# Two weight chunks side by side: gate and up products in turn into two PSUM tiles

## The chip, the core and the metric

The kernel runs on one core of a Trainium2 chip, as one launch. The metric is the device time of an execution in microseconds (us). Five engines run their own instruction streams and wait for each other by semaphores: TensorE (PE in the profile; PEld is its loading of weights), VectorE (DVE), ScalarE (ACT), GpSimd (POOL) and SyncE (SP), which here issues the weight loads from HBM. Matrix products are summed in PSUM tiles, which ScalarE and VectorE read.

## The reference

One inference step of a two-layer backbone over 384 tokens (256 latent, 128 context) of width 1024. Each layer is a feed-forward, a mixing block (a gated MLP over chunks of tokens beside differential attention) and a second feed-forward; each of the three is modulated by scales, shifts and gates that come from a conditioning vector.

```python
def swiglu(h, w13, w2):
    gate, up = jnp.split(h @ w13, 2, axis=-1)
    return (jax.nn.silu(gate) * up) @ w2

mod = jax.nn.silu(cond) @ w_mod[l] + b_mod[l]
sh1, sc1, gt1, sh2, sc2, gt2, sh3, sc3, gt3 = jnp.split(mod, N_MOD, axis=-1)
h = rmsnorm(x, g_norm[l, 0]) * (1.0 + sc1) + sh1
x = x + 0.5 * gt1 * swiglu(h, ffn1_w13[l], ffn1_w2[l])
...
h = rmsnorm(x, g_norm[l, 2]) * (1.0 + sc3) + sh3
x = x + 0.5 * gt3 * swiglu(h, ffn2_w13[l], ffn2_w2[l])
```

D_FF is 2816, 22 columns of 128; a layer runs for the context under one conditioning vector and for the latents under another.

## The kernel before

Everything is kept transposed: 128 features on the partitions, 384 tokens along the free dimension, 8 such blocks for a width of 1024. All weights come in chunks of 128 x 1024 floats (512 KB), one DMA each (L149) into one of seven `raw` buffers. To keep precision in TensorE's fast float format, each operand is split in a high and a low half: for weights ScalarE writes the high half `whi` (L180) and VectorE the low half `wlo` (L183), four buffers of each; activations are held in the same way. A 128-deep step of a product is then three matmuls into the same PSUM tile (`mm3`, L232 to L234): high by high, low weight by high, high weight by low.

The program is a list of jobs. A job is a generator that yields after each such step; the driver `step` takes them one after another and after each yield runs what was deferred (`run_later`): the low half of a weight chunk four steps after its high half, the low half of an activation one step after. The order in which the jobs issue is the order of every engine's stream.

A feed-forward is such a list. First some leading columns, in groups that also prepare the normalised input (`start_group` in the very first, `lead` in the others), then for each of the other gate and up columns (chunks c = 4 to 43 in the first feed-forward, 8 to 43 in the others) one `col_job`: it fetches its chunk, asks for the split of the chunk three further on, runs 8 steps (24 matmuls of 384 columns) into one PSUM tile out of four (`ps_mm`), and evacuates it. The evacuation of a gate column is a Silu on ScalarE (L713) into `t`; that of an up column multiplies `t` by the PSUM tile on VectorE (L732) and splits the product (copy on ScalarE L408, low half on VectorE L411). Then 22 jobs of w2 chunks follow, which sum eight output columns over 22 steps each and update `x`.

Beside the matmuls the kernel computes the conditioning for later stages, on VectorE. A piece (`mod_piece`, one of the nine 1024-wide parts) takes ten jobs: 0 to 7 read one `raw` chunk each and add it to two accumulators (job 0: L437, the others L439, two instructions each), job 8 reduces both (L445, tile `red`), and job 9 begins with a small matmul on TensorE that reads `red` into the tile `ms` (L450) and then writes the result with VectorE (L454). These jobs are put between the column jobs by `mods.put`: in three of the four feed-forwards 26 of them are spread over the chunks c = 8 to 43 and 14 more follow in w2, one per job; in the last one 10 are spread. A `mods` job issues its instructions at once and yields nothing.

Of the kernel before, what the change touches and what calls it, by code (L numbers as in the profile page):

```python
# [15 lines left out]
P = 128  # L16
D = 1024
KD = 8
NT = 384
# [21 lines left out]
def hybrid_step(  # L41
# [5 lines left out]
    T, V, S, G = nc.tensor, nc.vector, nc.scalar, nc.gpsimd  # L47
# [5 lines left out]
    def ps_mm():  # L53
        return pp.tile([P, 512], F32, tag="mm", name="mm", bufs=4)

    def tmp(w=NT):
        return sp.tile([P, w], F32, tag="t", name="t", bufs=5)
# [28 lines left out]
    def duo(p):  # L86

        return tuple(slot(2 * p + n, [P, KD, NT], F32R) for n in range(2))
# [21 lines left out]
    split_of = {}  # L110
    st = {"loaded": 0, "done": 0, "split": 0, "job": 0, "cur": None}
# [41 lines left out]
    def raw_done(key):  # L153
        del raw_of[key]
        gone.add(key)
        while st["done"] < st["loaded"] and order[st["done"]] in gone:
            st["done"] += 1
        load_next()
# [3 lines left out]
    def defer(fn, n):  # L162
        later.append([n, fn])

    def run_later(n=1):

        for e in later:
            e[0] -= n
        while later and later[0][0] <= 0:
            later.pop(0)[1]()  # L170

    def split_upto(c):
        c = min(c, len(chunks) - 1)
        while st["split"] <= c:
            i = st["split"]
            key = chunks[i]
            raw = raw_of[key]
            hi = sp.tile([P, 1024], F32R, tag="whi", name="whi", bufs=W_BUFS)
            lo = sp.tile([P, 1024], F32R, tag="wlo", name="wlo", bufs=W_BUFS)
            S.activation(out=hi, in_=raw, func=AF.Copy)  # L180

            def low(hi=hi, lo=lo, raw=raw, key=key):
                V.tensor_tensor(out=lo, in0=raw, in1=hi.bitcast(F32), op=ALU.subtract)  # L183
                raw_done(key)
            defer(low, LO_LAG)
            split_of[i] = (hi, lo)
            st["split"] += 1

    def w_get(c):
        if c >= st["split"] - 1:  # L190
            split_upto(c)
            run_later(99)
        split_upto(c + W_BUFS - 1)
        return split_of.pop(c)
# [36 lines left out]
    def mm3(ps, w_hi, w_lo, r_hi, r_lo, first, last):  # L231
        T.matmul(ps, lhsT=w_hi, rhs=r_hi, start=first, stop=False)  # L232
        T.matmul(ps, lhsT=w_lo, rhs=r_hi, start=False, stop=False)  # L233
        T.matmul(ps, lhsT=w_hi, rhs=r_lo, start=False, stop=last)  # L234

    def col_job(key, rhs, evac, n=NT, beside=()):

        def gen(c):
            hi, lo = w_get(c)
            ps = ps_mm()  # L240
            r_hi, r_lo = rhs()
            for kt in range(KD):
                sl = slice(kt * P, (kt + 1) * P)
                mm3(ps[:, :n], hi[:, sl], lo[:, sl], r_hi[:, kt, :], r_lo[:, kt, :], kt == 0, kt == KD - 1)
                for at, f in beside:
                    if at == kt:
                        f()
                yield
            evac(ps[:, :n])
        Job([key], gen)  # L250

    def lead_group(keys, evacs, l, i):


        def gen(c):
            n = len(keys)
            split_upto(c + n)
            run_later(99)
            ws = [split_of.pop(c + e) for e in range(n)]
            pss = [ps_mm() for _ in range(n)]  # L260
            r_hi, r_lo = rhs_u()
            seq = [(e, kt) for kt in range(5) for e in range(n)]
            seq += [(e, kt) for e in range(n) for kt in range(5, KD)]
            for at, (e, kt) in enumerate(seq):
                if at == 6:
                    norm_stats()
                if at == 14:
                    norm_bcast()
                sl = slice(kt * P, (kt + 1) * P)
                hi, lo = ws[e]  # L270
                mm3(pss[e][:, :NU], hi[:, sl], lo[:, sl], r_hi[:, kt, :], r_lo[:, kt, :], kt == 0, kt == KD - 1)
                if kt == KD - 1:
                    evacs[e](pss[e][:, :NU])
                    split_upto(c + n + 1 + e)
                yield
        Job(keys, gen)
# [130 lines left out]
    def split_act(dst_hi, dst_lo, src, lag=1):  # L407
        S.activation(out=dst_hi, in_=src, func=AF.Copy)  # L408

        def low():  # L410
            V.tensor_tensor(out=dst_lo, in0=src, in1=dst_hi.bitcast(F32), op=ALU.subtract)  # L411
        if lag:
            defer(low, lag)
        else:
            low()
# [199 lines left out]
    def normed(ps, out):  # L615

        b = tiny(2, "yb")
        V.tensor_copy(out=b, in_=ps[:, NT:NU])
        V.tensor_tensor(out=out, in0=ps[:, 0:NT], in1=nst["rb"], op=ALU.mult)
        return b  # L620
# [75 lines left out]
    def ffn(l, i, w13, w2, mods, after, n13):  # L696
        g = {}
        pc_sh, pc_gt = 3 * i, 3 * i + 2
        first = (l, i) == (0, 0)

        def g_tile(f):
            b = f // 8
            if b not in g:
                g[b] = duo(role["ZXW"[b]])
            return g[b][0][:, f % 8, :], g[b][1][:, f % 8, :]

        s_of = {}

        def gate_evac(f, u):
            def e(ps):  # L710
                s = s_of[f] = tmp()
                if not u:
                    S.activation(out=s, in_=ps, func=AF.Silu)  # L713
                    return
                b = normed(ps, s)
                for n, s0, s1 in TOK:
                    S.activation(out=s[:, s0:s1], in_=s[:, s0:s1], func=AF.Silu, bias=b[:, n:n + 1])
            return e

        def up_evac(f, u):  # L720
            def e(ps):
                s = s_of.pop(f)
                hi, lo = g_tile(f)
                if u:
                    t = tmp()
                    b = normed(ps, t)
                    for n, s0, s1 in TOK:
                        V.scalar_tensor_tensor(
                            out=s[:, s0:s1], in0=t[:, s0:s1], scalar=b[:, n:n + 1], in1=s[:, s0:s1],
                            op0=ALU.add, op1=ALU.mult)  # L730
                else:
                    V.tensor_tensor(out=s, in0=s, in1=ps, op=ALU.mult)  # L732
                split_act(hi, lo, s)
            return e

        n_u = 0 if first else 8
        n_0 = 4 if first else n_u
        keys, evs = [], []
        for f in range(NFF):
            keys += [(w13, l, f, 0), (w13, l, f, 1)]  # L740
            evs += [gate_evac(f, 2 * f < n_u), up_evac(f, 2 * f < n_u)]
        if first:
            start_group(keys[:n_0], rhs_h, evs[:n_0], make_h0(l, i, pc_sh))
        else:
            Job([], lambda c: iter_once(turn))
            lead(keys[:n_0], evs[:n_0], l, i, pc_sh)
        spread = 2 * NFF - 8
        for c in range(n_0, 2 * NFF):
            col_job(keys[c], rhs_h, evs[c])
            if first and c in (n_0, n_0 + 4):  # L750
                Job([], lambda c, f=small_loads if c == n_0 else lambdas: iter_once(f))
            if c >= 8:
                e = c - 8
                mods.put((e + 1) * n13 // spread - e * n13 // spread)

        pst = {}

        def mk(ci):
            def gen(c):
                hi, lo = w_get(c)  # L760
                for t in range(8):
                    dt, kt = divmod(ci * 8 + t, NFF)
                    if kt == 0:
                        pst["ps"] = ps_mm()
                    ps = pst["ps"]
                    sl = slice(t * P, (t + 1) * P)
                    a_hi, a_lo = g_tile(kt)
                    mm3(ps[:, :NT], hi[:, sl], lo[:, sl], a_hi, a_lo, kt == 0, kt == NFF - 1)
                    if after is None and (dt, kt) == (KD - 1, 12):
                        final_sums(0)  # L770
                    yield
                    if kt == NFF - 1:
                        update_x(l, pc_gt, dt, ps[:, :NT], after)
            return gen
        for ci in range(NFF):
            Job([(w2, l, ci // 2, ci % 2)], mk(ci))
            if ci < 16:
                mods.put()
        assert not mods.todo
# [345 lines left out]
    def iter_once(f):  # L1125
        f()
        return iter(())
# [157 lines left out]
```

## Time and profile before

| | |
|---|---|
| time, median of 3 runs | 1919.38 us (1918.47 to 1919.88) |
| the profiled execution's own time | 1918.23 us |
| its span, first to last instruction | 1916.2 us |
| mean granted TensorE clock | 0.997 |
| TensorE busy | 1903.4 us, 99% of the span |
| VectorE busy | 1308.7 us, 68% |
| ScalarE busy | 789.7 us, 41% |
| GpSimd busy | 198.5 us, 10% |
| weight chunks split (whi, wlo) | 424 |
| three-fold steps (L232, L233, L234) | 3136 of each |

The share of busy time of TensorE is from overlapping matmul records, whose ends are modelled; what a matmul costs is therefore read from the distance between the starts of neighbours. In the rows of the timeline the first number is the start of an instruction in us from the start of the span, the second its duration; in brackets stands how long its engine was idle before it and what ended that. In the table by windows a row has, for each engine, busy time and the number of instructions, then the granted TensorE clock, the DMA engines' busy share and GB/s. In the list of waits a row has the total, how often, and the longest.

### The profile page before, as it was taken

How to read it: one execution, taken by the hardware profiler on the slowest of the kernel's cores; microseconds unless marked ns; L12 is line 12 of the kernel's file. 1: busy time of each engine (PE TensorE's matmuls, PEld its weight loads, DVE VectorE, ACT ScalarE, POOL GpSimd, SP SyncE). 2: the span in 40 equal slices, each digit the busy share in tenths (PEclk: the TensorE clock that was granted, in tenths of full speed). 3: DMA queues.
4: the chain of work that ended last, by engine and by line, in shares of the span. 5: the costliest groups of instructions: out<-in, count | busy, mean ns of one | idle time of the engine just before them, and what ended most of it. 6: DMA issues, size and time to landing. Idle time of an engine off the chain costs nothing.

```text
span 1916.2 us, 28408 instructions
## 1 busy us (share of the span) xinstructions
PE 1903.4 (99%) x11024; PEld 1849.4 (97%) x11024; DVE 1308.7 (68%) x1948; ACT 789.7 (41%) x1412; POOL 198.5 (10%) x399
## 2 busy tenths in 40 slices
PE   8999999999999999999999999999999999999998
PEld 7999999889999999999999999998899999999998
DVE  5677885777656768778768779668766546655543
ACT  4433334445553444333334333354555534433332
POOL 0000003101221031000040000050022200400000
PEclk9999999999999999999999999999999999999999
DMA  8666663643335536566536656546433333354430
GB/s 331 197 200 194 219 207 128 214 131 112 98 100 173 162 112 201 189 197 223 181 109 221 192 192 223 170 137 200 123 111 103 102 123 130 111 172 157 154 110 34
DMA packets 91719, 308.69 MB, mean 161 GB/s; under 512 B 10816, under 2 KB 17600, under 8 KB 90816
## 3 DMA queue, kind: packets, MB, share of 16 engines
q1 hardware_dynamic: 90864, 306.17, 49.0%
q8 instruction: 87, 1.43, 0.3%
q10 hardware_dynamic: 720, 0.70, 0.1%
q14 instruction: 48, 0.39, 0.1%
HBM read 303.16 MB, written 3.67 MB: 160 GB/s over the span
## 4 chain that ended last, share of the span: by engine, by line
PE 98%; DMA 1%; DVE 0%; ACT 0%; issue 0%; DVEq 0%; ACTq 0%
PE mm L232 29%; PE mm L233 28%; PE mm L234 28%; PE mm L388 2%; PE mm L390 2%; PE mm L389 2%; PE sc L1009 2%; PE mm L1067 1%; PE tp L1050 1%; DMA S<-in_w_mod 1%; PE tp L835 1%; DMA gnorm<-in_g_norm 0%; PE ms L1096 0%; PE sc L301 0%; PE tp L640 0%; DMA cond<-in_cond 0%
## 5 line engine op out<-in xcount | busy, mean ns | idle before, releaser
L232 PE MATMUL mm<-S,whi 128*128 128x384 f32 (+1 forms) x3136 | 1063.8, 339 | 1.2 <-ACT S L560 1.2
L233 PE MATMUL mm<-S,wlo 128*128 128x384 f32 (+1 forms) x3136 | 1054.2, 336 | 0.2 <-DVE wlo L183 0.2
L234 PE MATMUL mm<-S,whi 128*128 128x384 f32 (+1 forms) x3136 | 1048.7, 334 | 0.0
L183 DVE TENSOR_TENSOR wlo<-raw,whi 128x1024 fp32r<-128x1024 f32 x424 | 520.6, 1229 | 239.9 <-ACT whi L180 239.2
L232 PEld LDWEIGHTS mm<-S,whi 128*128 128x128 f32 x3136 | 589.5, 188 | 14.0 <-issue 10.0
L234 PEld LDWEIGHTS mm<-S,whi 128*128 128x128 f32 x3136 | 588.8, 188 | 0.4 <-DVE S L563 0.4
L233 PEld LDWEIGHTS mm<-S,wlo 128*128 128x128 f32 x3136 | 587.6, 187 | 0.8 <-DVE wlo L183 0.6
L180 ACT ACTIVATE whi<-raw 128x1024 fp32r<-128x1024 f32 x424 | 445.5, 1052 | 199.6 <-PE mm L234 116.5
L439 DVE SCALAR_TENSOR_TENSOR acc<-raw,scond,acc 128x1024 f32<-128x1024 f32 x224 | 277.3, 1280 | 0.0
L408 ACT ACTIVATE S<-t 128x384 fp32r<-128x384 f32 x144 | 74.1, 523 | 329.7 <-DVE t L732 241.3
L509 POOL TENSOR_TENSOR yr<-yv,nhalf 128x3 f32<-128x3 f32 x9 | 9.6, 1062 | 1344.0 <-DVE yv L529 1016.6
L411 DVE TENSOR_TENSOR S<-t,S 128x384 fp32r<-128x384 f32 x144 | 83.8, 590 | 34.6 <-ACT S L408 34.6
L732 DVE TENSOR_TENSOR t<-t,mm 128x384 f32<-128x384 f32 x76 | 42.1, 554 | 77.8 <-PE mm L234 77.8
L713 ACT ACTIVATE t<-mm 128x384 f32<-128x384 f32 x76 | 37.3, 491 | 137.5 <-PE mm L234 137.5
L388 PE MATMUL mm<-whi,S 128*128 128x512 f32 x192 | 77.3, 403 | 0.0
L390 PE MATMUL mm<-whi,S 128*128 128x512 f32 x192 | 75.2, 392 | 0.0
L389 PE MATMUL mm<-wlo,S 128*128 128x512 f32 x192 | 75.1, 391 | 0.0
L577 POOL TENSOR_SCALAR t<-t,amod,modT 128x256 f32<-128x256 f32 x80 | 67.3, 850 | 4.2
L502 ACT ACTIVATE t<-x 128x384 f32<-128x384 f32 x44 | 22.9, 526 | 98.3 <-DVE x L627 98.3
L1100 DVE SCALAR_TENSOR_TENSOR S<-ms,sublng,S 128x128 fp32r<-128x128 f32 (+1 forms) x32 | 13.4, 418 | 65.3 <-ACT S L1099 65.3
L1026 ACT ACTIVATE e<-sc,ym 128x384 f32<-128x384 f32 (+1 forms) x96 | 47.7, 508 | 20.0 <-DVE ym L1016 20.0
L627 DVE SCALAR_TENSOR_TENSOR x<-mm,modT,x 128x256 f32<-128x256 f32 x96 | 35.6, 413 | 28.3 <-PE mm L234 28.0
(150 smaller groups left out, 1144.0 us busy)
## 6 DMA issues: line engine op xcount, KB each, us to landing
raw<-in_ffn_w SPq DMA_DIRECT2D x264, 512.0 KB, 4.2
raw<-in_w_mod SPq DMA_DIRECT2D x132, 512.0 KB, 4.6
raw<-in_w_in SPq DMA_DIRECT2D x112, 512.0 KB, 3.8
raw<-in_w_branch_a SPq DMA_DIRECT2D x16, 512.0 KB, 3.7
raw<-in_w_branch_b SPq DMA_DIRECT2D x16, 512.0 KB, 3.7
raw<-in_w_out SPq DMA_DIRECT2D x16, 512.0 KB, 3.7
S<-in_w_mod SPq DMA_DIRECT2D x6, 1024.0 KB, 10.7
x<-in_x SPq DMA_DIRECT2D x4, 384.0 KB, 4.2
```

What stands on the lines that cost most here:

```text
L180: S.activation(out=hi, in_=raw, func=AF.Copy)
L183: V.tensor_tensor(out=lo, in0=raw, in1=hi.bitcast(F32), op=ALU.subtract)
L232: T.matmul(ps, lhsT=w_hi, rhs=r_hi, start=first, stop=False)
L233: T.matmul(ps, lhsT=w_lo, rhs=r_hi, start=False, stop=False)
L234: T.matmul(ps, lhsT=w_hi, rhs=r_lo, start=False, stop=last)
L388: T.matmul(ps, lhsT=l_hi[:, kt, ts_], rhs=hi[:, sl], start=first, stop=False)
L389: T.matmul(ps, lhsT=l_hi[:, kt, ts_], rhs=lo[:, sl], start=False, stop=False)
L390: T.matmul(ps, lhsT=l_lo[:, kt, ts_], rhs=hi[:, sl], start=False, stop=last)
L408: S.activation(out=dst_hi, in_=src, func=AF.Copy)
L411: V.tensor_tensor(out=dst_lo, in0=src, in1=dst_hi.bitcast(F32), op=ALU.subtract)
L439: V.scalar_tensor_tensor(out=acc[n], in0=raw, scalar=s, in1=acc[n], op0=ALU.mult, op1=ALU.add)
L577: G.tensor_scalar(out=t[:, s0:s1], in0=t[:, s0:s1], scalar1=amod[:, i, kt, n:n + 1], scalar2=modT[:, l, pc_sh, kt, n:n + 1], op0=ALU.mult, ...
```

## The change

The column jobs of the gate and up weights are taken two at a time. A new job, `pair_job`, has both chunks, c and c+1, and two PSUM tiles; each of the three kinds of product is done for the gate's chunk and then for the up's, so that neighbours write different tiles. Both tiles are evacuated at the end of the job. It yields after every third product, as before. It asks for the split of chunks c+2 and c+3 when it begins. The conditioning jobs that the loop puts after chunk c and after chunk c+1 both come after the pair.

```diff
+    def pair_job(keys, rhs, evacs):
+
+        def gen(c):
+            if c + 1 >= st["split"] - 1:
+                split_upto(c + 1)
+                run_later(99)
+            ws = [split_of.pop(c + e) for e in range(2)]
+            split_upto(c + 3)
+            pss = [ps_mm()[:, :NT] for _ in range(2)]
+            r_hi, r_lo = rhs()
+            for kt in range(KD):
+                sl = slice(kt * P, (kt + 1) * P)
+                at = 0
+                for n, (w, r) in enumerate(((0, r_hi), (1, r_hi), (0, r_lo))):
+                    for e in range(2):
+                        T.matmul(
+                            pss[e], lhsT=ws[e][w][:, sl], rhs=r[:, kt, :],
+                            start=kt == 0 and n == 0, stop=kt == KD - 1 and n == 2)
+                        at += 1
+                        if at == 3:
+                            yield
+                if kt == KD - 1:
+                    for e in range(2):
+                        evacs[e](pss[e])
+                yield
+        Job(keys, gen)
...
         for c in range(n_0, 2 * NFF):
-            col_job(keys[c], rhs_h, evs[c])
+            if c % 2 == 0:
+                pair_job(keys[c:c + 2], rhs_h, evs[c:c + 2])
             if first and c in (n_0, n_0 + 4):
                 Job([], lambda c, f=small_loads if c == n_0 else lambdas: iter_once(f))
             if c >= 8:
```

The new lines move those below them: L438 is the L411 of before, L464, L466, L472, L477 and L481 are L437, L439, L445, L450 and L454, and L740 and L759 are L713 and L732.

The first place is VectorE's order in the first feed-forward, around the end of its first conditioning piece. `t` is the product of gate and up, `S7` the low half of it, `acc` the accumulators and `red` their reduction. Before:

```order
L439 SCALAR_TENSOR_TENSOR acc_758<-raw_965,scond_71,acc_758 128x1024
L439 SCALAR_TENSOR_TENSOR acc_759<-raw_965,scond_71,acc_759 128x1024
L411 TENSOR_TENSOR S7_1051<-t_1090,S6_1050 128x384
L183 TENSOR_TENSOR wlo_1130<-raw_999,whi_1129 128x1024
L445 TENSOR_REDUCE red_1163<-acc_758 128x32
L445 TENSOR_REDUCE red_1163<-acc_759 128x32
L183 TENSOR_TENSOR wlo_1167<-raw_1017,whi_1166 128x1024
L732 TENSOR_TENSOR t_1161<-t_1161,mm_1169 128x384
L454 TENSOR_TENSOR modT_78<-ms_1199,bmod_72 32x16 x4
```

With the change:

```order
L183 TENSOR_TENSOR wlo_1123<-raw_995,whi_1122 128x1024
L183 TENSOR_TENSOR wlo_1126<-raw_1000,whi_1125 128x1024
L759 TENSOR_TENSOR t_1186<-t_1186,mm_1129 128x384
L438 TENSOR_TENSOR S7_1041<-t_1186,S6_1040 128x384
L472 TENSOR_REDUCE red_1191<-acc_753 128x32
L472 TENSOR_REDUCE red_1191<-acc_754 128x32
L481 TENSOR_TENSOR modT_78<-ms_1194,bmod_72 32x16 x4
L183 TENSOR_TENSOR wlo_1202<-raw_1070,whi_1201 128x1024
```

Jobs 8 and 9 of the piece, which had a low half and a whole chunk's `t` between them, now follow each other behind one `t`.

The second place is TensorE's order at the matmul of job 9 that belongs to it. Before:

```order
L232 MATMUL mm_1169<-S0_150,whi_1058 128x384
L233 MATMUL mm_1169<-S0_150,wlo_1059 128x384
L234 MATMUL mm_1169<-S1_151,whi_1058 128x384
L450 MATMUL ms_1199<-red_1163,tiled_81 128x64
L232 MATMUL mm_1209<-S0_150,whi_1092 128x384
L233 MATMUL mm_1209<-S0_150,wlo_1093 128x384
L234 MATMUL mm_1209<-S1_151,whi_1092 128x384
```

With the change:

```order
L267 MATMUL mm_1129<-S1_151,whi_1052 128x384
L477 MATMUL ms_1194<-red_1191,tiled_81 128x64
L267 MATMUL mm_1207<-S0_150,whi_1122 128x384
L267 MATMUL mm_1208<-S0_150,whi_1125 128x384
L267 MATMUL mm_1207<-S0_150,wlo_1123 128x384
L267 MATMUL mm_1208<-S0_150,wlo_1126 128x384
```

Neighbouring products now write two tiles in turn. The small matmul stands ahead of the same two chunks as before, and the tile that VectorE multiplies ahead of `red` (mm_1129) is now the one written just before it.

The third place is VectorE's order from the last `t` of the same stage on, where the w2 chunks begin. Before:

```order
L732 TENSOR_TENSOR t_1972<-t_1972,mm_1981 128x384
L439 SCALAR_TENSOR_TENSOR acc_1788<-raw_1867,scond_71,acc_1788 128x1024
L439 SCALAR_TENSOR_TENSOR acc_1789<-raw_1867,scond_71,acc_1789 128x1024
L411 TENSOR_TENSOR S5_1641<-t_1972,S4_1640 128x384
L183 TENSOR_TENSOR wlo_2016<-raw_1887,whi_2015 128x1024
```

With the change:

```order
L759 TENSOR_TENSOR t_1997<-t_1997,mm_1940 128x384
L438 TENSOR_TENSOR S5_1631<-t_1997,S4_1630 128x384
L466 SCALAR_TENSOR_TENSOR acc_1783<-raw_1883,scond_71,acc_1783 128x1024
L466 SCALAR_TENSOR_TENSOR acc_1784<-raw_1883,scond_71,acc_1784 128x1024
L466 SCALAR_TENSOR_TENSOR acc_1783<-raw_1885,scond_71,acc_1783 128x1024
L466 SCALAR_TENSOR_TENSOR acc_1784<-raw_1885,scond_71,acc_1784 128x1024
L183 TENSOR_TENSOR wlo_2007<-raw_1881,whi_2006 128x1024
L183 TENSOR_TENSOR wlo_2010<-raw_1888,whi_2009 128x1024
```

Two conditioning jobs and two low halves stand behind this `t`, where one of each stood; the low half of `t` itself comes ahead of the conditioning jobs instead of behind them.

## The prediction

> **What bounds the kernel now.** I read the busy shares and the chain first, then the waits of the matmul engine, then its pace.
>
> ```profile
> PE 1903.4 (99%) x11024; PEld 1849.4 (97%) x11024; DVE 1308.7 (68%) x1948; ACT 789.7 (41%) x1412; POOL 198.5 (10%) x399
> PE 98%; DMA 1%; DVE 0%; ACT 0%; issue 0%; DVEq 0%; ACTq 0%
> ...
> PE sc L301 <- DMA S<-in_w_mod: 2.5, 2, 1.8
> PE mm L232 <- ACT S L560: 1.2, 2, 0.7
> PE tp L640 <- DVE ones L1168: 1.0, 1, 1.0
> PE mm L233 <- DVE wlo L183: 0.2, 1, 0.2
> ...
> 60.00:226.00 166.00, 166.00 (x960) 166.00 (x960) 127.34 (x147) 60.36 (x81) 0.00 (x0) 1.00 0.62 201
> ```
>
> TensorE (PE) is 98% of the chain that ended last, and it waits 4.9 us in all, all of it before 60 us. In the gate and up stage (60 to 226 us) 960 products take 166 us, 172.9 ns from start to start, at granted clock 1.00; VectorE (DVE) is busy 127.3 of those 166 us, 77%. So the time can fall only if a product takes less than 172.9 ns, and it rises by every wait that TensorE acquires. The change touches both.
>
> **The pace of a product.** 74 pairs are formed (20 in the first feed-forward, 18 in each of the other three), so 74 x 48 = 3552 products now switch PSUM tile every time. The kernel has switches already: its lead group goes to another tile after each third product (L234 to L232), and the 512-wide token-major products do the same (L390 to L388).
>
> ```profile
> 307.83 0.34 PE L232 MATMUL mm<-S,whi 128*128 128x386 f32 x1
> 308.01 0.34 PE L233 MATMUL mm<-S,wlo 128*128 128x386 f32 x1
> 308.19 0.34 PE L234 MATMUL mm<-S,whi 128*128 128x386 f32 x1
> 308.36 0.34 PE L232 MATMUL mm<-S,whi 128*128 128x386 f32 x1
> 308.54 0.34 PE L233 MATMUL mm<-S,wlo 128*128 128x386 f32 x1
> 308.71 0.34 PE L234 MATMUL mm<-S,whi 128*128 128x386 f32 x1
> 308.88 0.34 PE L232 MATMUL mm<-S,whi 128*128 128x386 f32 x1
> ...
> 349.96 0.39 PE L388 MATMUL mm<-whi,S 128*128 128x512 f32 x1
> ...
> 351.79 0.39 PE L390 MATMUL mm<-whi,S 128*128 128x512 f32 x1
> ```
>
> Across a switch (308.19 to 308.36, 308.71 to 308.88) the step is 0.17 us; on the same tile it is 0.17 to 0.18. A switch neither gains nor costs what these rows can resolve. The widths give a second bound: eight steps of 512 columns take 1.83 us, 228.8 ns each, so 128 more columns cost 55.9 ns, 0.437 ns each, and 384 of them 167.7 ns. Only 5.2 ns of the 172.9 are not proportional to width. If alternation removed all of that, 3552 x 5.2 ns = 18.5 us would go; I take 0, by the rows of the switches, and keep 18.5 for the range.
>
> **What moves on the other engines.** The order is the larger part of this change. The two conditioning jobs that stood after chunks c and c+1 now both stand behind the pair (first place of the order shown with the change). Where they are the jobs numbered 8 and 9 of a piece, the reductions `red` come behind t of that same pair, and the matmul that reads them (ms) is the next on TensorE, which before had a whole chunk, 24 products, in between (second place). TensorE runs in order, so all products of the next pair queue behind ms, and the evacuations, and the SP queue's loads that wait for buffers, stand behind those. Of 26 conditioning jobs in the w13 stages of three feed-forwards, numbers 8 and 9 (of 0 to 9 in a piece) fall behind one pair twice each: 6 places. The fourth has 10 jobs, never two behind a pair.
>
> **The price of such a place.** Rows around a chunk's end:
>
> ```profile
> 98.67 0.56 DVE L732 TENSOR_TENSOR t<-t,mm 128x384 f32<-128x384 f32 x1 [0.24 <-PE mm L234]
> 99.82 0.56 DVE L411 TENSOR_TENSOR S<-t,S 128x384 fp32r<-128x384 f32 x1 [0.59 <-ACT S L408]
> ...
> 118.17 0.55 DVE L411 TENSOR_TENSOR S<-t,S 128x384 fp32r<-128x384 f32 x1
> 118.64 1.22 DVE L183 TENSOR_TENSOR wlo<-raw,whi 128x1024 fp32r<-128x1024 f32 x1
> 119.78 2.37 DVE L445 TRANSPOSE_TENSOR_REDUCE red<-acc 128x32 f32<-128x1024 f32 x2
> ...
> 119.10 0.33 PE L234 MATMUL mm<-S,whi 128*128 128x384 f32 x1
> 119.47 0.49 ACT L713 ACTIVATE t<-mm 128x384 f32<-128x384 f32 x1 [2.09 <-PE mm L234]
> ```
>
> Count from the start of the pair's last product. The gate's last product is one step earlier, so Silu starts at 0.37 - 0.17 = 0.20 and ends at 0.69; t right behind it, near 0.72; the low half (L411) 1.15 behind t, at 1.87; the next instruction 0.47 later, at 2.34; two reductions 2.37, so 4.71; ms starts then, or a little later, and not at 0.17. **4.6 us each, 27.6 us for six.** Before, this was hidden by the 24 products (4.15 us) between.
>
> **Behind pairs with two accumulating jobs** (five per feed-forward that can hit the next pair, 15 in all) VectorE has four accumulations ahead of the next pair's low halves (the third place of the order shows the same sequence):
>
> ```profile
> 215.62 0.55 DVE L732 TENSOR_TENSOR t<-t,mm 128x384 f32<-128x384 f32 x1 [0.24 <-PE mm L234]
> 216.09 2.48 DVE L439 SCALAR_TENSOR_TENSOR acc<-raw,scond,acc 128x1024 f32<-128x1024 f32 x2
> 218.48 0.55 DVE L411 TENSOR_TENSOR S<-t,S 128x384 fp32r<-128x384 f32 x1
> ...
> 229.54 2.36 DVE L445 TRANSPOSE_TENSOR_REDUCE red<-acc 128x32 f32<-128x1024 f32 x2
> ...
> 232.15 0.33 PE L450 MATMUL ms<-red,tiled 128*128 128x64 f32 x2
> ```
>
> Two accumulations step 2.39 us (216.09 to 218.48), a low half 1.14 (118.64 to 119.78). So 2.34 + 4.78 + 1.14 + 1.22 = 9.48 us for the second wlo, which the fourth product of the next pair wants at 0.17 + 51 x 0.173 = 9.0. With the weight load ahead of the product: 0.5 to 0.7, **0.6 x 15 = 9.0 us**. In the old order each wlo had three chunks of lead. One accumulating job behind a pair ends at 2.34 + 2.39 + 1.14 + 1.22 = 7.1 us and costs nothing.
>
> **At the start of w2** the same delay reaches the third piece (third place of the order): behind the last t of the stage stand four accumulations and two low halves, where two and one stood. Two accumulations (2.39) and one low half (1.14) more, 0.68 of wait for the copy and 0.35 for Silu: 4.6 us later. The reductions ended at 231.90 and ms came at 232.15, a slack of 0.25. About 4.2 us at three places, **12.6 us**; the fourth w2 has no such job.
>
> **The first pair** (chunks 4, 5) begins with two chunks, but ScalarE splits chunk 5 only behind the copy of the pair before:
>
> ```profile
> 48.73 0.34 PE L233 MATMUL mm<-S,wlo 128*128 128x384 f32 x1
> ...
> 49.84 2.95 ACT L180 ACTIVATE whi<-raw 128x1024 fp32r<-128x1024 f32 x3
> ...
> 50.92 4.75 DVE L183 TENSOR_TENSOR wlo<-raw,whi 128x1024 fp32r<-128x1024 f32 x4 [0.40 <-ACT whi L180]
> ```
>
> The second product now waits from 48.7 to 50.9 for whi, the fourth from 51.2 to 52.15 for wlo: **3.0 us**, once. Everything else (evacuations, two PSUM tiles per pair of four, loads of raw) lies beside products: DMA share 0.62 in this stage.
>
> **The clock.** Nine of these pauses last over 4 us. The trace has one spell of half clock:
>
> ```profile
> 9.40:12.90 3.50, 2.80 (x28) 2.21 (x26) 0.47 (x3) 0.00 (x0) 0.87 (x1) 0.89 1.01 394
> ...
> 11.50:12.00 0.50, 0.50 (x10) 0.21 (x9) 0.16 (x1) 0.00 (x0) 0.07 (x1) 1.00 0.90 359
> 12.00:12.50 0.50, 0.21 (x4) 0.00 (x0) 0.00 (x0) 0.00 (x0) 0.50 (x1) 0.60 1.03 378
> 12.50:18.50 6.00, 5.58 (x35) 3.56 (x36) 2.98 (x11) 2.61 (x4) 0.30 (x1) 0.50 1.03 410
> 18.50:19.00 0.50, 0.50 (x5) 0.50 (x4) 0.47 (x2) 0.26 (x1) 0.00 (x0) 0.58 0.97 410
> ...
> 17.51 3.07 PE L640 MATMUL tp<-ones 128*128 128x128 f32 x20
> 24.52 1.50 PE L301 MATMUL sc<-S,scond 128*32 128x256 f32 x24 [1.75 <-DMA S<-in_w_mod]
> 24.00:26.00 2.00, 1.48 (x25) 0.72 (x25) 2.00 (x2) 0.60 (x1) 0.00 (x0) 1.00 1.01 422
> ```
>
> It lasted 6.8 us (12.1 to 18.9) and ended 1.4 us after an unbroken run of matmuls began at 17.51; an idle 1.75 us at 22.8 did not lower the clock. Bounds per pause: 0, or half of 6.8 us, 3.4, together 0 to 31 us. Here full-width products follow each pause at once, so I am nearest to the 1.4 us row: half clock over 1.4 to 2 us loses 0.7 to 1.0; 1.0 x 9 = **9 us**.
>
> The Trainium skill's TensorE: Matmul & The Clock Gate (Part 1) says that the clock halves after an idle window of some 3.4 us, that the windows run freely, and that as long a busy one restores it. The trace agrees in length (6.8 us is two such windows). By that rule a pause of 4.6 us holds a whole idle window in about a third of its positions and then loses 1.7 us, an estimate of 5 us for nine instead of 9.
>
> **Sum.** 27.6 + 9.0 + 12.6 + 3.0 + 9 = 61.2 us, on the profiled execution's own 1918.2 us (span 1916.2 and 2.0 around it): 1979.4 us. The median of the runs, 1919.4, is 1.1 higher, well inside the error of the sum.
>
> **Rivals.**
> - *The clock holds.* No drop at all: 1918.2 + 52.2 = 1970. For it: 1.75 us idle did not trip it. Against: a stretch of thin work (28 records in the 3.5 us from 9.4) did.
> - *Each pause costs the whole spell:* 52.2 + 31 gives 2001. Against: the spell of the trace had thin work in it to prolong it.
> - *Waits overlap and part of the sum is counted twice* (VectorE catches up during a 4.6 us pause, the 0.6 us waits vanish, and w2 costs half): 27.6 + 6.3 + 3.0 = 36.9, so 1955.
> - *The same-tile sum is what holds the pace, and alternating removes it.* Place: the 3552 products; 18.5 us off gives 1961. For an end below 1918 it must remove 61.2 us / 3552 = 17.2 ns, three times the 5.2 that the widths leave; at 25 ns the time would be 1979 - 89 = 1890. Against it stand the steps of 0.17 at switches. That the products would not alternate at all is excluded by the order above.
>
> The same page (Back-to-back issue gap) gives columns / 2.4 + 2.5 ns, 162.5 for 384; the trace has 172.9. If those 10.4 ns were the price of one tile, an estimate of 37 us off would give 1942, still slower.
>
> **Chances.** Forecast 1979 (about 1966 to 1994 of its own): 0.50; clock holds 0.20; whole spells 0.08; counted twice 0.13; alternation gains 5 ns 0.04; alternation gains over 17 ns 0.03; otherwise near no change 0.02. About 0.2% (3.8 us) is what a measurement of this kernel can tell from none. Faster 0.03, the same 0.02, slower 0.95. The range 1950 to 1998 leaves out the fastest and most of the whole-spell case.
>
> **What would show it.** In the profile after: six waits of ms for red of 4 to 5 us in the w13 stages and three in w2; some fifteen waits of a product for wlo of about half a microsecond; 172 to 174 ns per product in a stretch of pairs without a wait; granted clock below 1.00 behind the long pauses. The prediction is wrong if ms does not wait, or if undisturbed pairs run below 168 ns or above 178 ns a product.

## The result and the profile after

The changed kernel takes 1998.9 us (median of 4 runs, 1998.27 to 1999.92) against 1919.2: a ratio of 1.0417 with a 95% interval of 1.0404 to 1.043. It is slower, as forecast, by 79.7 us where 61 were forecast, and 0.9 us above the end of the range. The profiled execution has a span of 1997.8 us, 81.6 more than before; the accounts below are made in that span.

The page of the profile after, and its core:

```profile
PE 1935.6 (97%) x11024; PEld 1870.1 (94%) x11024; DVE 1307.2 (65%) x1948; ACT 788.7 (39%) x1412; POOL 197.9 (10%) x399
```

```profile
core 0: 1997.8 us, clock 0.984
```

TensorE's waits after, which answer to those shown of before (total, how often, longest):

```profile
PE ms L477 <- DVE red L472: 39.8, 9, 4.5
PE mm L267 <- DVE wlo L183: 7.7, 19, 0.6
PE mm L267 <- ACT whi L180: 2.9, 4, 2.0
PE mm L232 <- ACT S L587: 1.2, 2, 0.7
```

VectorE and ScalarE are as busy as before (1307 and 789 us). TensorE has the same 11024 records, but waits 50 us that it did not wait: nine times for `red`, nineteen times for a low half, four times for a high half. The granted clock fell from 0.997 to 0.984.

The first of the nine places in the timeline of TensorE after:

```profile
128.84 0.51 PE L267 MATMUL mm<-S,whi 128*128 128x384 f32 x2
133.77 0.43 PE L477 MATMUL ms<-red,tiled 128*128 128x64 f32 x2 [4.42 <-DVE red L472]
134.02 0.84 PE L267 MATMUL mm<-S,whi 128*128 128x384 f32 x2
134.66 0.84 PE L267 MATMUL mm<-S,wlo 128*128 128x384 f32 x2
...
138.79 0.52 PE L267 MATMUL mm<-S,whi 128*128 128x384 f32 x2
139.15 0.51 PE L267 MATMUL mm<-S,wlo 128*128 128x384 f32 x2
...
145.39 0.51 PE L267 MATMUL mm<-S,wlo 128*128 128x384 f32 x2
```

and of ScalarE and VectorE:

```profile
129.21 0.49 ACT L740 ACTIVATE t<-mm 128x384 f32<-128x384 f32 x1 [5.07 <-PE mm L267]
...
129.74 0.55 DVE L759 TENSOR_TENSOR t<-t,mm 128x384 f32<-128x384 f32 x1 [2.23 <-ACT t L740]
130.88 0.56 DVE L438 TENSOR_TENSOR S<-t,S 128x384 fp32r<-128x384 f32 x1 [0.59 <-ACT S L435]
131.35 2.36 DVE L472 TRANSPOSE_TENSOR_REDUCE red<-acc 128x32 f32<-128x1024 f32 x2
```

The last product starts at 129.01 (the second of the two from 128.84). Counted from there, Silu starts at 0.20, `t` at 0.73, its low half at 1.87, the reductions at 2.34, and `ms` at 4.76: the chain of the prediction to 0.05 us. But then two products take 0.64 us (134.02 to 134.66), 320 ns each; from 139.15 on, 36 products take 6.24 us, 173.3 ns each. Windows over this place and the next two show why (behind the busy times of the five engines stands the granted clock, 0.54 over the slow stretch, then 1.00):

```profile
134.00:137.75 3.75, 3.75 (x14) 3.75 (x14) 3.15 (x7) 0.00 (x0) 0.00 (x0) 0.54 0.05 9
138.00:139.00 1.00, 1.00 (x8) 1.00 (x7) 0.00 (x0) 0.00 (x0) 0.00 (x0) 1.00 0.87 307
199.25:206.00 6.75, 6.14 (x20) 6.17 (x21) 3.59 (x8) 0.00 (x0) 0.00 (x0) 0.51 0.29 93
257.25:264.00 6.75, 5.97 (x20) 6.00 (x21) 4.88 (x9) 0.00 (x0) 0.00 (x0) 0.51 0.53 168
```

Taken in windows of a quarter of a microsecond over the whole execution, half clock is granted in ten spells behind pauses, each of 3.4 or of 6.8 us, 54.6 us together; 8.4 us of them lie inside the pauses, 46.2 on products.

Where a spell begins and ends can be read from the same trace. The spells of one execution all begin whole multiples of 3.413 us apart. Here are slots of that length, cut at these times, at the first and the sixth place (behind the comma TensorE's busy time, then the granted clock in the slot):

```profile
130.77:134.19 3.42, 0.42 (x3) 1.00 0.41 168
134.19:137.60 3.41, 3.41 (x13) 0.50 0.01 2
...
936.32:939.73 3.41, 1.48 (x9) 1.00 0.94 358
939.73:943.15 3.42, 1.02 (x4) 0.50 0.35 126
943.15:946.56 3.41, 3.41 (x13) 0.50 0.60 187
```

At the first place one slot is idle for 3.00 us, the next runs at half clock, and as it has no idle time the clock is full again behind it. At the sixth place a slot's edge cuts the pause in 1.93 and 2.40 us: the clock drops at the edge, the first slow slot is itself idle in part, and a second one follows. Between the first 60 and the last 12 us the profiled executions of the two kernels and of the ten experiments have no exception to this: a slot with 1.85 us or more of idle time was followed by half clock (43 slots), one with 1.73 or less was not; half clock ended behind a slot with at most 0.39 us idle (43) and went on behind one with 0.43 or more (22). So it is the place of the pause on this grid, not only its length, that sets the price. The grid was read from the traces afterwards; no run was made to move a pause on it.

The first pair of a later feed-forward, which the prediction did not price:

```profile
752.20 0.34 PE L267 MATMUL mm<-S,whi 128*128 128x384 f32 x1
752.82 0.44 PE L267 MATMUL mm<-S,whi 128*128 128x384 f32 x1 [0.28 <-ACT whi L180]
753.10 0.34 PE L267 MATMUL mm<-S,wlo 128*128 128x384 f32 x1
754.08 0.44 PE L267 MATMUL mm<-S,wlo 128*128 128x384 f32 x1 [0.64 <-DVE wlo L183]
```

Three steps here take 1.88 us instead of 0.52. The step behind such a wait, and behind each of the 15 waits inside the stages, is 0.28 us instead of 0.17, which the list of waits doesn't count. The account of the 81.6 us, by terms:

| term | forecast | measured | from |
|---|---|---|---|
| `ms` behind `red`, nine places | 27.6 + 12.6 | 41.3 | 39.8 of idle time and 0.17 each by which a start comes later than the idle time says (at the first place 4.76 from start to start, 4.59 more than a usual step, for 4.42 idle) |
| 15 waits for `wlo` | 9.0 | 9.2 | 0.68 from start to start, and 0.28 for the step behind, instead of 0.17 each |
| first pair of all | 3.0 | 3.2 | 2.38 + 0.28 + 0.98 + 0.28 less four usual steps |
| first pairs of the other three | 0 | 4.4 | 1.36 + 1.33 + 1.43, and 0.11 each for the step behind |
| second pairs of the other three | 0 | 0.9 | one step of 0.36 to 0.41 and one of 0.28 in each |
| half clock | 9 | 21.1 | 46.2 us x (1 - 173.9 / 320) |
| pace of the 3552 products | 0 | 1.5 | mean step at full clock, steps over 190 ns left out: 173.89 ns in the pairs, 173.46 in the same stages before |
| sum | 61.2 | 81.6 | the span is 81.6 longer; the terms are good to some tenths, so the exact agreement is chance |

### The profile page after: what moved, and what is told of

It is laid out like the page before. It is cut to its first block, busy times and chain, and to the rows that moved or that the text cites. A ratio compares the mean times of both kernels' runs of the same rounds, so it can differ in the third digit from the quotient of the medians.

```text
span 1997.8 us, 28432 instructions
## 1 busy us (share of the span) xinstructions
PE 1935.6 (97%) x11024; PEld 1870.1 (94%) x11024; DVE 1307.2 (65%) x1948; ACT 788.7 (39%) x1412; POOL 197.9 (10%) x399
## 3 DMA queue, kind: packets, MB, share of 16 engines
q8 instruction: 87, 1.43, 0.3%
## 5 line engine op out<-in xcount | busy, mean ns | idle before, releaser
L232 PE MATMUL mm<-S,whi 128*128 128x384 f32 (+1 forms) x1952 | 667.6, 342 | 1.2 <-ACT S L587 1.2
L233 PE MATMUL mm<-S,wlo 128*128 128x384 f32 (+1 forms) x1952 | 659.9, 338 | 0.5 <-DVE wlo L183 0.5
L234 PE MATMUL mm<-S,whi 128*128 128x384 f32 (+1 forms) x1952 | 656.3, 336 | 0.0
L183 DVE TENSOR_TENSOR wlo<-raw,whi 128x1024 fp32r<-128x1024 f32 x424 | 513.8, 1227 | 185.6 <-ACT whi L180 185.2
L267 PE MATMUL mm<-S,whi 128*128 128x384 f32 x2368 | 519.9, 341 | 2.9 <-ACT whi L180 2.9
L180 ACT ACTIVATE whi<-raw 128x1024 fp32r<-128x1024 f32 x424 | 437.1, 1049 | 201.6 <-PE mm L234 109.3
L267 PEld LDWEIGHTS mm<-S,whi 128*128 128x128 f32 x2368 | 427.9, 191 | 4.2 <-ACT whi L180 4.2
L232 PEld LDWEIGHTS mm<-S,whi 128*128 128x128 f32 x1952 | 369.2, 189 | 14.0 <-issue 10.0
L234 PEld LDWEIGHTS mm<-S,whi 128*128 128x128 f32 x1952 | 368.7, 189 | 0.6 <-DVE S L590 0.6
L267 PE MATMUL mm<-S,wlo 128*128 128x384 f32 x1184 | 313.0, 343 | 7.8 <-DVE wlo L183 7.7
L466 DVE SCALAR_TENSOR_TENSOR acc<-raw,scond,acc 128x1024 f32<-128x1024 f32 x224 | 275.8, 1280 | 0.0
L740 ACT ACTIVATE t<-mm 128x384 f32<-128x384 f32 x76 | 37.3, 491 | 393.4 <-PE mm L267 392.3
L759 DVE TENSOR_TENSOR t<-t,mm 128x384 f32<-128x384 f32 x76 | 42.0, 553 | 184.5 <-ACT t L740 182.8
L438 DVE TENSOR_TENSOR S<-t,S 128x384 fp32r<-128x384 f32 x144 | 84.1, 591 | 62.8 <-ACT S L435 62.8
```

Of the source, the lines that this page charges most:

```text
L267: T.matmul(pss[e], lhsT=ws[e][w][:, sl], rhs=r[:, kt, :], start=kt == 0 and n == 0, stop=kt == KD - 1 and n == 2)
L466: V.scalar_tensor_tensor(out=acc[n], in0=raw, scalar=s, in1=acc[n], op0=ALU.mult, op1=ALU.add)
```

## The experiments

Theory A was: alternation is worth nothing; the loss is TensorE's waits for work that the new order puts late, and the half clock behind them. Its rivals: that alternating itself costs (B) or saves (C) some 5 ns a product, and that what lies beyond the waits is not the clock.

### The pairs, but by threes

```diff
-                for n, (w, r) in enumerate(((0, r_hi), (1, r_hi), (0, r_lo))):
-                    for e in range(2):
+                for e in range(2):
+                    for n, (w, r) in enumerate(((0, r_hi), (1, r_hi), (0, r_lo))):
```

> Pairs as in the change, with every wait and every conditioning job where it stands, but the three products of a step go to one PSUM tile before the other tile gets its three (switch after every third product, not after each). Theory A (alternation itself is worth nothing; the 80 us are waits of TensorE and the half clock behind them): 1993 to 2000 us, at most 2.6 us below the change, since the second low half is wanted by the fifth product instead of the fourth. Rival B (alternating costs about 5 ns a product): 1999 - 18 = 1981. Rival C (alternating saves 5 ns, hidden under the waits): 2017.

Measured: 1988.5 us, ratio 1.0365 (1.0348 to 1.0382), 10.4 us below the change and 4.5 below the expectation of A. The waits:

```profile
PE ms L477 <- DVE red L472: 37.2, 9, 4.2
PE mm L267 <- DVE wlo L183: 3.3, 4, 0.8
```

The expectation was that each of the 15 waits for `wlo` inside the stages gets 0.17 us shorter; they are gone from the list. The gate's tile is finished three products ahead of the up's and not one, so Silu, `t` and all that follows on VectorE come 0.3 us earlier (the longest wait for `red` fell from 4.5 to 4.2), and the low half is wanted 0.17 later; together that is more than the 0.36 of idle time. A little is left at these places, steps of up to 0.24 and 0.28 us, so some 6.8 of the 9.2 us went there, and 2.6 in the waits for `red`: 9.4 of the 10.4 us between the medians. (The profiled execution is the slowest of the four, 1994.1 us; it has 6.8 us more of half clock than the change, all of it in the first 61 us.) The undisturbed pace is 173.88 ns, as with alternation (173.89), which speaks against B and C. So alternation, product by product, has a price here, but by what it does to the times of other engines.

### Job 9 one pair later

```diff
+        late, held, behind, put = {}, {}, [], [0]
...
-                mods.put((e + 1) * n13 // spread - e * n13 // spread)
+                for _ in range((e + 1) * n13 // spread - e * n13 // spread + late.pop(c, 0)):
+                    if c % 2 and behind and behind[-1] % 10 == 8 and behind[0] // 2 == c // 2 and put[0] % 10 == 9 and held.get(put[0]) is None:
+                        held[put[0]] = True
+                        late[c + 1] = 1
+                        continue
+                    behind[:] = [c, put[0]]
+                    mods.put()
+                    put[0] += 1
```

> The change, but where jobs 8 and 9 of a conditioning piece fall behind one pair, job 9 (the matmul ms) goes behind the next pair. Theory A: six waits of 4.5 us go (27 us) and with them six spells of half clock (30.7 us long together, about 14 us lost): 1999 - 41 = 1958 us; three waits of ms at the start of w2 stay. Rival (VectorE is simply too busy, and the wait moves on to wlo or to the later ms): above 1975.

Measured: 1959.2 us, ratio 1.0205 (1.0188 to 1.0222), 1 us off A. Six of nine waits went and no new one came:

```profile
PE ms L477 <- DVE red L472: 13.0, 3, 4.3
PE mm L267 <- DVE wlo L183: 7.7, 19, 0.6
PE mm L267 <- ACT whi L180: 3.0, 4, 2.0
```

Half of the loss is the place of one small matmul, with the clock behind it.

### The pauses filled

```diff
+        if nst.setdefault("piece", 0) in (0, 1, 2, 6, 7, 8, 10, 11, 12):
+            warm(18)
+        nst["piece"] += 1
         ps = pp.tile([P, 64], F32, tag="ms", name="ms")
         T.matmul(ps, lhsT=tiled, rhs=red.rearrange("p n b -> p (n b)"), start=True, stop=True)
```

> The change, with 18 products that nobody reads (128 columns, ones by ones, into a spare PSUM tile) put on TensorE ahead of each of the nine ms matmuls that wait, some 4.0 us of work in a wait of 4.5. The waits for red stay as long. Theory A (the part of the loss beyond the waits, about 26 us, is the clock that halves behind a pause): granted clock 1.00 there, nine spells of 51 us together gone, 51 x 0.46 = 23 us saved: 1973 to 1980 us. Rival (the excess is not the clock): 1996 to 2001, or more if the added products overrun.

Measured: 1983.9 us, ratio 1.0333 (1.0318 to 1.0349), 15.0 us below the change. The idle time at the nine places went from 39.8 to 3.6 us, `ms` starts no earlier, and the clock holds. The wait, and windows at the first place:

```profile
PE ms L480 <- DVE red L472: 3.6, 9, 0.5
```

```profile
133.00:137.00 4.00, 4.00 (x37) 4.00 (x36) 2.71 (x4) 2.91 (x4) 0.00 (x0) 1.00 0.70 243
137.00:139.00 2.00, 1.60 (x11) 1.41 (x11) 1.40 (x6) 0.00 (x0) 0.00 (x0) 1.00 0.00 0
139.00:141.00 2.00, 2.00 (x13) 2.00 (x12) 1.73 (x3) 0.00 (x0) 0.00 (x0) 1.00 0.01 4
```

All nine spells are gone, so the clock is shown as the cause of that part. The saving is less than the 19 to 26 us expected: in this execution the spell behind the first pair is 6.8 us long instead of 3.4 (1.6 us more), and one more of 3.4 us falls in the first 30 us, before the pairs. The nine spells, 51 us of which 8.4 lie in pauses, should give 19.5; 15.0 plus 1.6 and up to 1.6 are 17 to 18, and what became of the other 2 us stays open.

### Half of the filling

```diff
-            warm(18)
+            warm(9)
```

> The change with 9 instead of 18 unread products ahead of each of the nine waiting ms matmuls: 2 us of work, then some 2.5 us of idle time. It asks which pause lowers the clock. If only a pause over 3.4 us does, no spell of half clock at the nine places, 1984 us as with 18. If it is the share of idle time in a window of 3.4 us, some of the nine places still have a spell: 1988 to 1996.

Measured: 1987.7 us, ratio 1.0358 (1.0343 to 1.0374). The time lies just below the second range expected, and the spells decide for it: idle time is left at the nine places, 2.3 to 2.5 us each, and five of the nine have a spell, each of 3.4 us. The first place in the timeline, and the slots of 3.413 us around the first and the second:

```profile
132.45 0.69 PE L480 MATMUL ms<-red,tiled 128*128 128x64 f32 x2 [2.42 <-DVE red L472]
```

```profile
128.69:132.10 3.41, 1.34 (x13) 1.00 0.50 202
132.10:135.52 3.42, 3.07 (x10) 0.50 0.01 2
...
193.54:196.96 3.42, 2.34 (x20) 1.00 0.77 279
196.96:200.37 3.41, 1.99 (x12) 1.00 0.00 1
200.37:203.78 3.41, 3.41 (x22) 1.00 0.45 155
```

So a pause well under 3.4 us can lower the clock, and the same pause at another place does not: at the first place 2.07 us of it lie in one slot, at the second 1.08 and 1.42 on the two sides of an edge. The five slots ahead of a spell have 1.85 us or more of idle time, at the other four places no slot has more than 1.48.

### Alternation with the other work spread again

The conditioning jobs of chunk c and the split of chunk c+3 in the middle of each pair, and single jobs for the first two chunks of a stage:

```diff
-            split_upto(c + 3)
+            split_upto(c + 2)
...
+                if kt == 3:
+                    for go, ks in mid:
+                        go()
+                    split_upto(c + 3)
...
```

> Alternation on 3360 products without the moved work: in each pair the conditioning jobs of chunk c and the split of chunk c+3 stand in the middle of the pair, those of c+1 at its end, as far apart as in the kernel before; the first two chunks of each stage stay single. Theory A: alternation is worth nothing, no pause over 1 us: 1916 to 1923 us. Rival C (a product on a fresh tile saves the 5.2 ns that widths leave): 1919 - 17 = 1902. Rival B (costs 5 ns): 1936.

Measured: 1943.9 us, ratio 1.013 (1.0114 to 1.0145). None of the three expectations held. The waits show that the edit did not do what it was meant to:

```profile
PE ms L481 <- DVE red L476: 6.8, 3, 2.3
PE mm L267 <- DVE wlo L183: 5.9, 13, 0.9
PE mm L267 <- ACT whi L180: 2.0, 3, 0.7
```

Three waits at the start of w2, thirteen for low halves, and two spells of half clock remain. The pace of its undisturbed pairs is 173.88 ns, and that answers the question which the total does not: neither 5 ns less nor 5 ns more.

### The grouping alone, without pairs

The kernel before with only this edit:

```diff
-            if c >= 8:
-                e = c - 8
-                mods.put((e + 1) * n13 // spread - e * n13 // spread)
+            if c >= 8 and c % 2:
+                e = c - 9
+                mods.put((e + 2) * n13 // spread - e * n13 // spread)
```

> The kernel before, with single column jobs and no alternation; only the conditioning jobs of two chunks are put together behind the second. Theory A (the moved order alone makes the waits): ms waits for red at the six places, from 0.84 us (t, one step behind the chunk's end) + 2.37 = 3.2 us on, instead of 0.17: 3.0 us each, 18 us; at the start of w2 two accumulations more, 2.39 less the slack of 0.25, 2.1 us at three places, 6.4 us: 1944 us, and up to 15 us more if the clock halves behind pauses of 2 to 3 us. Low halves keep three chunks of lead, so no waits for wlo. Rival (alternation and the two tiles make the loss): 1917 to 1923.

Measured: 1955.6 us, ratio 1.0185 (1.017 to 1.02).

```profile
PE ms L450 <- DVE red L445: 24.3, 9, 3.0
```

24.3 us of waits where 24.4 were worked out, and no wait for a low half. Six of the nine pauses, of 2.1 to 3.0 us, have a spell (one of 6.8, five of 3.4 us, 24 us together), which is some 10 us. The three without one are 2.9 to 3.0 us long, longer than three of those with one (2.1 to 2.2); but they are cut by an edge of the grid, with at most 1.73 us in one slot. So the grouping alone, without any product being moved, costs 36 us, where the whole change costs 80.

### Pairs that begin four chunks later

```diff
-            if c % 2 == 0:
+            if c < n_0 + 4:
+                col_job(keys[c], rhs_h, evs[c])
+            elif c % 2 == 0:
                 pair_job(keys[c:c + 2], rhs_h, evs[c:c + 2])
```

> The change, but the first four chunks of each stage after the lead stay single column jobs, so that the first pair finds its halves ready. Theory A: the waits of the first pairs go (3.1 us in the first feed-forward and 1.4 us in each of the other three) and one spell of half clock of 3.4 us (1.6 lost): 1999 - 8.9 = 1990 us. The ms waits and the spells behind them stay.

Measured: 1992.4 us, ratio 1.0382 (1.0365 to 1.0399), 6.5 us below the change instead of 8.9. The waits for `whi` and four of the 19 for `wlo` are gone. The nine spells left behind pauses are as long together (54.6 us) as the ten of the change, since more of them are of the long kind; whether that is the missing 2.4 us was not tried.

### All of it mended

The two edits before (job 9 later, pairs later), and at the start of w2 one place without a conditioning job between jobs 8 and 9:

```diff
             if ci < 16:
-                mods.put()
+                if n13 == 26 and put[0] == 29 and not held.get("w2"):
+                    held["w2"] = True
+                else:
+                    mods.put()
+                    put[0] += 1
```

> Alternation kept; job 9 one pair later, also one w2 chunk later at the start of w2, and the first four chunks of each stage single. The sum of the parts: of 80 us stay the 15 waits for wlo (7.8 us) and a pace of 173.85 instead of 173.5 ns (1.2 us): 1928 us (1925 to 1933). If it is clearly above, a part of the loss has not been found; if it is below 1919, alternation gains.

Measured: 1935.7 us, ratio 1.0086 (1.0071 to 1.0101); 63 of the 80 us are gone, 8 fewer than expected.

```profile
PE mm L267 <- DVE wlo L183: 5.1, 15, 0.4
PE ms L477 <- DVE red L472: 4.3, 6, 1.3
```

No spell of half clock behind any pause. The shift in w2 has left six small waits for `red`, three of which (1.2 to 1.3 us) are at the second piece there, where before the slack was 0.45. Of the 17.3 us in the span, 15 waits for `wlo` with the step behind each are 9.2, the six for `red` 4.3 and 0.17 each, the pace 1.4; about 1.4 are left.

### The mended kernel, with `wlo` last, and by threes

```diff
-                for n, (w, r) in enumerate(((0, r_hi), (1, r_hi), (0, r_lo))):
+                for n, (w, r) in enumerate(((0, r_hi), (0, r_lo), (1, r_hi))):
```

> The mended kernel (job 9 later, first four chunks single) with alternation kept, but the products by the low half of the weight come last in each step, so the second wlo is wanted by the sixth product and not by the fourth: 0.35 us of each of the 15 waits for wlo goes, 5.2 us: 1930.5 us against 1935.7. Rival (the remaining 16 us are alternation itself, not these waits): unchanged, 1935 to 1937.

and, instead of it, the loops turned round as in the first experiment:

> The mended kernel with pairs, but three products to one tile, then three to the other. As between the change and its version by threes, the 15 waits for wlo vanish (7.8 us): 1928 us against 1935.7; the rest above 1919 is the waits of ms in w2 (some 6 us) and 1 to 3 us not accounted for. Rival (writing the tiles in turn gains what these waits hide): above 1935.7.

Measured: 1930.45 us, ratio 1.0061 (1.0046 to 1.0076), and 1925.75 us, ratio 1.0033 (1.0021 to 1.0046). Neither list has a wait for `wlo` in the pairs any more; the first row of each is

```profile
PE ms L477 <- DVE red L472: 4.0, 4, 1.3
```

with `wlo` last, and

```profile
PE ms L477 <- DVE red L472: 3.8, 3, 1.3
```

by threes. The first keeps the alternation and moves only what is wanted when, and saves the 5.2 us that were worked out; steps of up to 0.35 and 0.28 us are left at the 15 places. The second writes one tile three times in a row and is the fastest of all kernels with pairs; its pace is 173.47 ns, where the first kernel by threes had 173.88, so the tenths of a nanosecond above the 173.46 of before follow no order of the tiles. No version tried beats the kernel before.

## Why the prediction was wrong, point by point

- **The pace.** Right: the steps of 0.17 us at tile switches said that alternation is worth nothing, and in the pairs a product takes 173.89 ns instead of 173.46. Nothing of the 5.2, 10.4 or 17.2 ns of the rivals shows.
- **The six places in w13, 4.6 us each.** Right to a tenth of a microsecond; moving job 9 took 39.7 us away with what followed.
- **Behind pairs with two accumulating jobs, 0.6 x 15.** Right in place, number and size, 9.2 us in all. The kernels with `wlo` last and by threes show that the moment at which the product wants it is the other half of this wait.
- **The start of w2, 4.2 at three places.** Right: 4.3 us of idle time each, 4.5 from start to start beyond a usual step. (The prediction's own terms, 4.56 less 0.25, give 4.3.)
- **The first pair, 3.0 us.** Right with 3.2. "Once" was wrong: in the three later feed-forwards the first pairs wait 1.5 us each and the second ones 0.3. In the first of these, ScalarE's split of the second chunk stands behind a copy that waited 3.3 us for VectorE's last work on the leading columns; with pairs that begin four chunks later the waits are gone. The prediction read this place in one of four stages only: 5.3 us missed.
- **"Here full-width products follow each pause at once, so I am nearest to the 1.4 us row": this is the step that failed.** Its 1.0 us for each of nine pauses measured 2.1 for each of ten. That the clock halves behind the pauses was right and was shown by filling them, but a spell does not end 1.4 us after dense work begins: it lasts one slot or two, 3.4 or 6.8 us, and ends only at the end of a slot with almost no idle time. The row for the length was in the prediction's own fence (6.8 us) and was set aside for the shorter one. (The trace before has a second spell, from 1913.3 us to its end, where TensorE has no work left; it bears on none of these places.) The term was 12 us too small, of the 20.4 by which the account exceeds the sum; the later first and second pairs are 5.3 more.
- **The Trainium skill's rule** (TensorE: Matmul & The Clock Gate, Part 1). The lengths agree: 3.41 and 6.83 us are one and two of its windows, and all spells of an execution begin on one grid of that step. That only a whole idle window lowers the clock does not: nine of nine pauses of 4.3 to 4.5 us had a spell, where it gives a third, pauses of 2.3 to 2.5 us had one in five of nine, and 1.85 idle us of 3.41 were enough. The measurement decides.
- **The rivals.** Counted twice: no, the waits add up as forecast. The clock holds: no. The whole spell at each pause: nearest, with 2001 us, and given 0.08; but in part by luck, since its 3.4 us a pause is more than the 2.1 measured, and that made up for the waits of the later feed-forwards, which it lacks too.

## What to carry to other kernels

When jobs that issue to several engines are merged, look first at what stood between them: here a reduction on VectorE and the matmul that reads it had 24 products between them, and the merge, not the tiles, decided the time. Where TensorE is busy all the time, as here, a pause costs its length and what the clock takes afterwards. A new wait of 4 us brought a whole spell of half clock each time, 1.6 us lost for a short one and up to 3.1 for a long one; a wait of 2 to 3 us brought it or not, by where it lay, so both are to be in the range of a forecast. Whether a new order of products is faster in itself could here be read from the old trace: tile switches were there already, and took no less time than their neighbours.

## What the runs showed of the hardware that was not expected

- Half clock comes in spells of 3.41 or 6.83 us. Behind idle times of 4.0 to 4.5 us in the change and three experiments: 30 of 30. Of 2.1 to 3.0 us, in the grouping alone: six of nine. Of 2.3 to 2.5 us behind 2 us of narrow products: five of nine. Of 1.3 us and less, in the mended kernels: none. During a spell a 384-column product takes 320 ns instead of 173.
- The clock changes on a grid of 3.413 us. It dropped behind a slot with 1.85 us or more of idle time and never behind one with 1.73 or less, and it came back behind a slot with at most 0.39 us idle. So a spell begins inside the pause or up to 1.6 us behind it, and the products that pay for it are mostly those behind the pause.
- Writing two PSUM tiles in turn, product by product, takes 173.89 ns a product, three to a tile 173.88 and 173.47, all to one tile 173.46: nothing that one would order work for, in either direction.
